# Taps behind splits, gates' sums a projection later, residual sums in tiles of their own, and a last row tile finished on two engines

## The chip, the cores and the metric

The kernel runs on one core of one Trainium2 chip. The metric is the device time of one execution in microseconds (us), as the median of several runs. The core has five engines with a queue each: TensorE (PE, matmuls and transposes), VectorE (DVE), ScalarE (ACT), GpSimd (POOL) and SyncE (SP), which in this kernel issues all DMAs. Each engine takes its instructions strictly in order. They wait for one another through semaphores.

## The reference

One layer of a decoder on 1024 tokens of width 1024, float32: a SwiGLU block, a token mixer, a second SwiGLU block, and a last RMSNorm.

```python
x = x + 0.5 * swiglu(rms_norm(x, ffn1_norm), ffn1_w_gate, ffn1_w_up, ffn1_w_down)
x = x + token_mixer(rms_norm(x, mix_norm), w_in, ...)
x = x + 0.5 * swiglu(rms_norm(x, ffn2_norm), ffn2_w_gate, ffn2_w_up, ffn2_w_down)
return rms_norm(x, final_norm)

def token_mixer(h, ...):
    p = h @ w_in
    ...
    y_a = pool_mixer(u_pool, pool_w, pool_scale)
    y_b = forgetting_attention(q, k, v, z_f, forget_bias)
    y_c = conformer_conv(h_glu, conv_w, conv_b, conv_ln_g, conv_ln_b)
    return concatenate([y_a, y_b, y_c]) @ w_out
```

The pool mixer takes trailing means over 2, 4, 8 and 16 tokens. The attention has 8 heads of 64 and a forget gate per head, whose log sigmoids are summed along the tokens. The convolution is causal and depthwise, 31 taps on 256 channels, on a gated input, with a LayerNorm behind it. The two SwiGLU blocks have 2816 hidden channels.

## The kernel before, in words

Every product is made in three matmuls: each operand is split into a high part (a cast on ACT) and a low part (the rest, a subtraction on DVE), by `split` (L77 to L80) or `split_scaled` (L82 to L85); high by high, high by low and low by high are summed in PSUM. So each operand that PE reads has had one ACT and one DVE instruction. PSUM tiles come from two tags: `bank` (four of 512 columns) and `banks` (two of 1024 columns). SBUF tiles come from four tags, of which `g2` has 11 buffers of 1024 columns; a new tile waits until the last reader of the tile that had its buffer is done, a DMA included.

The order on an engine comes from the order of the code, from a scheduler, and from two helpers: `in_order(start, *engines)` chains all instructions from `start` on in the order in which they are written, and `follow(i, j)` puts one instruction behind another.

The stages are these.

1. The first SwiGLU block (`ffn`, L339 to L562): 77 products of row blocks with pairs of gate and up weights, then 7 groups of down products, whose results are added to the row tiles `xs[0..7]`.
2. The projections of the mixer (from L743 on). `gate(c, h)` makes the gated input of the convolution. `pool_mm` and `pool` make the pooled channels; the latter has some ten DVE instructions, and ends in a split. A loop of 16 value tiles `vp` (256 columns of 8 heads' values, and the gates' logits) follows, then `qk(0)` to `qk(7)`, one per 128 rows of queries or keys, each of 48 matmuls in two halves. `qk` puts the result in a `banks` tile `pp`, and `qk_out` splits it: `qkh` on ACT, `qkl` on DVE. Since there are two such tiles, `qk(i)` can only start when `qkl` of `qk(i-2)` has been read out.
3. The convolution runs beside this on DVE: `conv(n)` issues the next n of 62 taps (31 for each of two channel halves, L719 and L721, tile `ua`). The calls of `conv` stand between the pieces of stage 2. `behind` with `follow` puts the next tap of a half behind the last split of a `pool`.
4. `log_sigmoid` makes the gates' logarithms in place (tile `gates`). `running_sum` turns them (8 transposes into `lp`), sums them on DVE in two scans (tile `fd`), splits the sum (tile `terms`), negates both parts on ACT and stores the rows in DRAM (`augq`, `augk`). It is called in the second half of `qk(2)`, ahead of that projection's `qk_out`. The last taps come in `qk(4)`, the LayerNorm's two means (`channel_mean`) behind `qk(4)` and `qk(5)`.
5. Attention over 64 steps, with output products of finished channels between them.
6. The residual loop (L1176 to L1197): for each of 8 row tiles, 12 matmuls `po`, whose result is added in place to `xs[t]` (L1185 or L1187), a store of `xs[t]` to DRAM (`kept`, L1188), the squares on ACT (`norm2.square`), and one tile later `norm2.scale`, which writes the scaled rows in place into `xs[t]` (L153). The reciprocal root comes from POOL in two small instructions (`inverse`, L147 and L148). From tile 2 on, the scaled rows of the tile two before are transposed (`turn`, tile `tp`, and two splits into `o11` and `o21`).
7. The second SwiGLU block, with weights loaded by `Pair.load` (four loads of two DMAs ahead of stage 6), and `prepare`, which splits them. Both products of `11` come first, then both of `21`. The row tiles are loaded again from `kept`.
8. `finish` (L1218 to L1233) normalises the last row tile in two halves.

In the residual loop before the change, the write of scaled rows has to wait for the store of the same tile:

```python
nc.vector.tensor_tensor(xs[t], o.rearrange("p c x -> p (c x)"), xs[t], op=ALU.add)
nc.sync.dma_start(kept[ts, :], xs[t])
norm2.square(t)
...
norm2.scale(t - 1)
```

## Time and profile before

| what | us |
|---|---|
| median of 3 runs | 1766.65 |
| lowest and highest run | 1762.13, 1768.06 |
| the profiled execution, its own time | 1767.13 |
| its span, first to last instruction | 1765.4 |
| PE busy | 1723.7 (98% of the span) |
| DVE busy | 1216.5 (69%) |
| ACT busy | 690.1 (39%) |
| POOL busy | 164.1 (9%) |
| mean granted clock of PE | 0.991 |

Line numbers, as L153, are those of the kernel before. A row of a timeline gives the start, the duration, engine, line, operation and tiles, and in brackets the idle time of the engine ahead of it with what ended it. Rows that are merged carry a count (x7). Two rows of one engine can overlap by about 0.1 us, so the pitch of equal instructions is a little under the duration of one. PE's rows show 0.39 us for a matmul of 512 columns, while the next begins 0.23 us later. The granted clock is 1.00 at 2.4 GHz and 0.50 at 1.2 GHz.

### The profile page before, as it was taken

Reading aid. Unit: us, or ns where it says so; the run is one execution under the profiler, and the core shown is the slowest. Engines: PE = TensorE matmul, PEld = TensorE weight load, DVE = VectorE, ACT = ScalarE, POOL = GpSimd, SP = SyncE. Lnnn points to the kernel's source line nnn. Section 1 sums busy time; section 2 is a strip of 40 time slices with the busy share of each in tenths; the row PEclk is TensorE's granted clock in tenths of the full one; section 3 lists DMA queues with packets and bytes.
Section 4 is the critical chain, followed back from the end, with each engine's and each line's share of the span. In section 5 each row is a group of like instructions: output and inputs, shape, how many; then the busy total and the mean of one; then the engine's idle time right before and its main releaser. Section 6 shows DMA issues by size and latency. Waiting matters only on the chain.

```text
span 1765.4 us, 21430 instructions
## 1 busy us (share of the span) xinstructions
PE 1723.7 (98%) x8213; PEld 1432.2 (81%) x8214; DVE 1216.5 (69%) x1465; ACT 690.1 (39%) x968; POOL 164.1 (9%) x218
## 2 busy tenths in 40 slices
PE   8999999999999999999899999899999999999998
PEld 6788888888888788898788887788888888888886
DVE  7766666555787674699567786876655566678676
ACT  5433333333334433222545664443333333334343
POOL 3000000000000100221134452100000000000010
PEclk9999999999999999999999999999999999999999
DMA  5333233335723323012563413252333332853342
GB/s 179 109 130 102 89 102 130 99 106 225 282 95 114 102 84 96 1 50 75 170 158 74 121 38 112 68 161 90 104 129 101 102 102 90 334 190 103 106 144 83
DMA packets 173687, 209.69 MB, mean 119 GB/s; under 512 B 9969, under 2 KB 116496, under 8 KB 173584
## 3 DMA queue, kind: packets, MB, share of 16 engines
q1 hardware_dynamic: 173584, 208.31, 36.9%
q8 instruction: 65, 1.06, 0.3%
q14 instruction: 38, 0.31, 0.1%
HBM read 150.87 MB, written 57.41 MB: 118 GB/s over the span
## 4 chain that ended last, share of the span: by engine, by line
PE 48%; DVE 7%; ACT 1%; issue 1%; DMA 1%; POOL 0%; DVEq 0%; POOLq 0%; ACTq 0%
PE pb L354 10%; PE pc L354 6%; PE pa L354 6%; PE po L529 4%; PE po L530 4%; PE po L531 4%; DVE ua L721 4%; PE ysum L1083 2%; PE ptp L1072 2%; PE po L192 1%; PE po L194 1%; PE po L193 1%; PE s L1035 1%; PE s L1036 1%; PE pp L192 1%; PE pp L193 1%
## 5 line engine op out<-in xcount | busy, mean ns | idle before, releaser
L354 PE MATMUL pb<-ot,hi 128*128 128x512 f32 x1056 | 329.9, 393 | 4.4 <-DVE ot L80 4.4
L80 DVE TENSOR_TENSOR lo<-a,hi 128x1024 fp32r<-128x1024 f32 x132 | 161.3, 1223 | 166.8 <-ACT hi L79 166.8
L529 PE MATMUL po<-dh,hh 128*128 128x512 f32 x616 | 240.6, 391 | 1.0 <-DVE x L537 1.0
L530 PE MATMUL po<-dl,hh 128*128 128x512 f32 x616 | 240.1, 390 | 0.0
L531 PE MATMUL po<-dh,hl 128*128 128x512 f32 x616 | 240.0, 390 | 0.0
L354 PEld LDWEIGHTS pb<-ot,hi 128*128 128x128 f32 x1056 | 199.7, 189 | 47.0 <-DVE ot L80 5.8
L79 ACT CAST hi<-a 128x1024 fp32r<-128x1024 f32 x132 | 139.2, 1055 | 250.3 <-PE pa L354 136.7
L354 PE MATMUL pa<-o,hi 128*128 128x512 f32 x704 | 217.7, 390 | 0.0
L354 PE MATMUL pb<-ot,lo 128*128 128x512 f32 x528 | 206.9, 392 | 0.0
L354 PEld LDWEIGHTS pa<-o,hi 128*128 128x128 f32 x704 | 131.6, 188 | 27.1
L147 POOL TENSOR_SCALAR rs<-ss 128x1 f32<-128x1 f32 x32 | 16.9, 529 | 1323.0 <-ACT xn L143 1275.5
L354 PE MATMUL pa<-o,lo 128*128 128x512 f32 x352 | 137.1, 390 | 1.6 <-DVE lo L80 1.6
L529 PEld LDWEIGHTS po<-dh,hh 128*128 128x128 f32 x616 | 116.0, 188 | 25.9 <-DVE x L537 1.8
L531 PEld LDWEIGHTS po<-dh,hl 128*128 128x128 f32 x616 | 115.9, 188 | 24.3
L79 ACT CAST dh<-ds 128x1024 fp32r<-128x1024 f32 (+1 forms) x60 | 58.9, 982 | 195.7 <-DVE ds L395 177.2
L530 PEld LDWEIGHTS po<-dl,hh 128*128 128x128 f32 x616 | 115.9, 188 | 23.8
L354 PEld LDWEIGHTS pb<-ot,lo 128*128 128x128 f32 x528 | 100.0, 189 | 20.8
L354 PE MATMUL pc<-ot,hi 128*128 128x512 f32 x352 | 108.7, 390 | 0.0
L354 PE MATMUL pc<-o,hi 128*128 128x512 f32 x352 | 108.4, 389 | 0.0
L80 DVE TENSOR_TENSOR dl<-ds,dh 128x1024 fp32r<-128x1024 f32 (+1 forms) x60 | 68.1, 1135 | 51.4 <-ACT dh L79 51.3
L80 DVE TENSOR_TENSOR hl<-hr,hh 128x1024 fp32r<-128x1024 f32 x84 | 95.0, 1131 | 2.3 <-PE po L530 0.8
L721 DVE SCALAR_TENSOR_TENSOR ua<-ua,cw 128x1023 f32<-128x1023 f32 (+29 forms) x60 | 88.3, 1491 | 0.6
(243 smaller groups left out, 3173.8 us busy)
## 6 DMA issues: line engine op xcount, KB each, us to landing
hr<-hid SPq DMA_DIRECT2D x70, 512.0 KB
a<-in_ffn_w_gate_dram SPq DMA_DIRECT2D x88, 256.0 KB
a<-in_ffn_w_up_dram SPq DMA_DIRECT2D x88, 256.0 KB
wd<-in_ffn_w_down_dram SPq DMA_DIRECT2D x8, 2048.0 KB
st<-qkd SPq DMA_DIRECT2D x48, 256.0 KB
hid<-ta SPq DMA_DIRECT2D x22, 512.0 KB
hid<-p SPq DMA_DIRECT2D x22, 512.0 KB
x<-in_x_dram SPq DMA_DIRECT2D x16, 512.0 KB
```

Of the source, the lines that this page charges most:

```text
L79: nc.scalar.copy(hi, src)
L80: nc.vector.tensor_tensor(lo, src, f32(hi), op=ALU.subtract)
L192: nc.tensor.matmul(o, wh, mh, start=(i == 0), stop=False)
L193: nc.tensor.matmul(o, wh, ml, start=False, stop=False)
L194: nc.tensor.matmul(o, wl, mh, start=False, stop=(i == n - 1))
L354: nc.tensor.matmul(o, a[:, m, k, :], r[:, b, k, :], start=(start and k == n == 0), stop=(k == 3 and n == 2), skip_group_check=not start,)
L529: nc.tensor.matmul(o[t], hh[:, k, ts], wh[:, k], start=(g == 0 and k == 0), stop=False)
L530: nc.tensor.matmul(o[t], hh[:, k, ts], wl[:, k], start=False, stop=False)
L531: nc.tensor.matmul(o[t], hl[:, k, ts], wh[:, k], start=False, stop=(g == 5 and k == n - 1))
L721: nc.vector.scalar_tensor_tensor(a[:, s:], u[:, :T - s], k, a[:, s:], op0=ALU.mult, op1=ALU.add)
L1072: nc.tensor.transpose(tp[:, k, i, :], items[head * NT + 2 * j + i][0][:, kt * P:(kt + 1) * P], ident)
L1083: nc.tensor.matmul(yp[:, j % 2, :], vs[key_tile(j, u, k)][:, head], pts[:, x % 4, s, k, :], start=(u == 0 and k == 0 and s == 0), stop=(u ...
```

## The change

There are four parts.

Taps. The two `gate` calls of the second channel half ask for 7 taps each instead of 3, and the four places in the pool stage ask for 2 and 1 instead of 4 and 3; `conv(7)` is issued behind `ready(2)`. In the value loop the tap stands behind the split instead of ahead of it.

Gates. `running_sum` keeps the transposes and the scans, and is called after `qk(2)` with its `qk_out`. The split of the sum, the negations and the stores are in `sum_terms`, called in the second half of `qk(3)`. The next tap of each half follows the last scan.

Residual loop. The sum goes to a tile `sums` of its own, out of `g2`. The store reads `sums`, the squares go to the dead `xs[t]` instead of a tile of their own, and `scale` reads `sums` and writes `xs[t]`. Only the first of the two weight halves of each pair is loaded ahead of the loop, the second behind tiles 3 and 5. The weights of both `11` products are prepared in the loop, those of both `21` products behind it. The DVE chain of the loop and of the block's first products is one `in_order` call (`begin` is handed to `ffn`), in both SwiGLU blocks.

Finish. Half 0 is multiplied by the gain on DVE before the root is known, then scaled on ACT and stored from ACT's queue. Half 1 is done on DVE and stored from SP's. The two partial sums of squares are added on POOL in the instruction that adds epsilon, not on DVE.

```diff
         def scale(self, t):
             rs = self.inverse(t)
-            nc.vector.scalar_tensor_tensor(self.xn[t], xs[t], rs, self.gain, op0=ALU.mult, op1=ALU.mult)
+            src = self.src.pop(t, xs[t])
+            nc.vector.scalar_tensor_tensor(self.xn[t], src, rs, self.gain, op0=ALU.mult, op1=ALU.mult)
...
-        def square(self, t):
-            self.xn[t] = xs[t]
+        def square(self, t, src=None):
+            self.xn[t], self.src[t] = xs[t], xs[t] if src is None else src
             self.ss[t] = small.tile([P, 1], F32, name="ss")
-            squares = slot("g2", F32, name="squares")
-            nc.scalar.activation(squares, xs[t], AF.Square, scale=D ** -0.5, accum_out=self.ss[t])
+            squares = slot("g2", F32, name="squares") if src is None else xs[t]
+            nc.scalar.activation(squares, self.src[t], AF.Square, scale=D ** -0.5, accum_out=self.ss[t])
...
-    gate(1, 0, None, lambda: conv(3))
+    gate(1, 0, None, lambda: conv(7))
...
-    gate(1, 1, None, lambda: (conv(3), ready(2)))
+    gate(1, 1, None, lambda: (ready(2), conv(7)))
...
-    pu = pool_mm(0, lambda h: (ready(3), fetch()) if h else conv(4))
+    pu = pool_mm(0, lambda h: (ready(3), fetch()) if h else conv(2))
...
-    pu = pool_mm(1, lambda h: conv(3) if h else ready(4))
+    pu = pool_mm(1, lambda h: conv(1) if h else ready(4))
...
-            conv(1)
             vv = vp[:, :256].rearrange("p (h c) -> p h c", c=HD)
             split(vs[t][:, 4 * j:4 * j + 4, 0, :], vs[t][:, 4 * j:4 * j + 4, 1, :], vv)
+            conv(1)
...
-        terms = slot("g2", F32R, name="terms")
+        behind.update({0: last_instruction(), 1: last_instruction()})
+        sums["fd"] = fd
+
+    def sum_terms():
+        fd, terms = sums["fd"], slot("g2", F32R, name="terms")
         fh, fl, nh, nl = (terms[32 * i:32 * i + HEADS, :] for i in range(4))
         split(fh, fl, fd)
...
-    qk(2, lambda: None, running_sum)
-    qk(3)
+    qk(2)
+    running_sum()
+    qk(3, lambda: None, sum_terms)
...
-    for i in range(4):
-        pairs2[i // 2].load(0, i % 2)
+    for pair in pairs2:
+        pair.load(0, 0)
...
+        sums = slot("g2", F32, name="sums")
...
-                nc.vector.tensor_tensor(xs[t][:, cs], oc, xs[t][:, cs], op=ALU.add)
+                nc.vector.tensor_tensor(sums[:, cs], oc, xs[t][:, cs], op=ALU.add)
         if t % 2 == 0:
-            nc.vector.tensor_tensor(xs[t], o.rearrange("p c x -> p (c x)"), xs[t], op=ALU.add)
-        nc.sync.dma_start(kept[ts, :], xs[t])
-        norm2.square(t)
+            nc.vector.tensor_tensor(sums, o.rearrange("p c x -> p (c x)"), xs[t], op=ALU.add)
+        nc.sync.dma_start(kept[ts, :], sums)
+        norm2.square(t, sums)
...
         if t in (3, 5):
-            pairs2[0].prepare(("11", "21")[t // 2 - 1])
+            pairs2[t // 2 - 1].prepare("11")
+            pairs2[t // 2 - 1].load(0, 1)
...
-    for n in ("11", "21"):
-        pairs2[1].prepare(n)
+    for pair in pairs2:
+        pair.prepare("21")
...
-        xn = slot("g2", F32, name="xn")
+        xn, squares = slot("g2", F32, name="xn"), slot("g2", F32, name="squares")
...
-        r.ss[t] = small.tile([P, 1], F32, name="ss")
-        nc.vector.tensor_tensor(r.ss[t], ss[:, 0:1], ss[:, 1:2], op=ALU.add)
-        rs = r.inverse(t)
-        for c in range(2):
-            nc.vector.scalar_tensor_tensor(xn[:, cs[c]], xs[t][:, cs[c]], rs, r.gain[:, cs[c]], op0=ALU.mult, op1=ALU.mult)
-            nc.sync.dma_start(out[t * P:(t + 1) * P, cs[c]], xn[:, cs[c]])
+        nc.vector.tensor_tensor(xn[:, cs[0]], xs[t][:, cs[0]], r.gain[:, cs[0]], op=ALU.mult)
+        rs = small.tile([P, 1], F32, name="rs")
+        nc.gpsimd.tensor_scalar(rs, ss[:, 0:1], ss[:, 1:2], EPS, op0=ALU.add, op1=ALU.add)
+        nc.gpsimd.tensor_tensor(rs, rs, mhalf, op=ALU.pow)
+        nc.scalar.activation(xn[:, cs[0]], xn[:, cs[0]], AF.Copy, scale=rs)
+        nc.vector.scalar_tensor_tensor(xn[:, cs[1]], xs[t][:, cs[1]], rs, r.gain[:, cs[1]], op0=ALU.mult, op1=ALU.mult)
+        nc.scalar.dma_start(out[t * P:(t + 1) * P, cs[0]], xn[:, cs[0]])
+        nc.sync.dma_start(out[t * P:(t + 1) * P, cs[1]], xn[:, cs[1]])
```

On DVE, from the split of `qk(1)`'s result to that of `qk(2)`'s, before (the last tap ahead of the scans on; `qkl` is a projection's low part, `fd` a scan, `terms` the split of the sum, `ua` a tap):

```order
L721 SCALAR_TENSOR_TENSOR ua<-ua,cw 128x999
L858 SCALAR_TENSOR_TENSOR fd<-one,lp 8x512
L721 SCALAR_TENSOR_TENSOR ua<-ua,cw 128x998
L858 SCALAR_TENSOR_TENSOR fd<-one,fd,lp 8x512
L721 SCALAR_TENSOR_TENSOR ua<-ua,cw 128x997
L80 TENSOR_TENSOR terms<-fd,terms 8x1024
L721 SCALAR_TENSOR_TENSOR ua<-ua,cw 128x996
L85 SCALAR_TENSOR_TENSOR qkl<-pp,qkh 128x1024
```

The same place on DVE now:

```order
L724 SCALAR_TENSOR_TENSOR ua<-ua,cw 128x1005
L85 SCALAR_TENSOR_TENSOR qkl<-pp,qkh 128x1024 x2
L863 SCALAR_TENSOR_TENSOR fd<-one,lp 8x512
L863 SCALAR_TENSOR_TENSOR fd<-one,fd,lp 8x512
L724 SCALAR_TENSOR_TENSOR ua<-ua,cw 128x1004
L724 SCALAR_TENSOR_TENSOR ua<-ua,cw 128x1003
L80 TENSOR_TENSOR terms<-fd,terms 8x1024
L724 SCALAR_TENSOR_TENSOR ua<-ua,cw 128x1002
```

The low parts of `qk(1)` and `qk(2)` now follow each other, with no tap between them and the scans behind them; before, seven taps, both scans, the split of the sum and three more taps stood between the two.

On ACT, at the same place, before (`wh` is a weight's high part, `qkh` a projection's):

```order
L182 CAST wh<-raw 128x1024
L79 CAST terms<-fd 8x1024
L84 ACTIVATE qkh<-pp 128x1024
L864 ACTIVATE terms<-terms 8x1024
L865 ACTIVATE terms<-terms 8x1024
```

And now:

```order
L183 CAST wh<-raw 128x1024
L84 ACTIVATE qkh<-pp 128x1024
L79 CAST terms<-fd 8x1024
L873 ACTIVATE terms<-terms 8x1024
L183 CAST wh<-raw 128x1024
```

The high part of `qk(2)` stood behind the cast that waits for the scans, and now stands ahead of it.

On SP, at the residual loop, before (`a_...` are weight halves, `kept` the stores of the row tiles):

```order
L295 DMA a_8614<-in_ffn_w_up_dram 128x4x128
L295 DMA a_8617<-in_ffn_w_gate_dram 128x4x128
L295 DMA a_8617<-in_ffn_w_up_dram 128x4x128
L295 DMA a_8620<-in_ffn_w_gate_dram 128x4x128
L295 DMA a_8620<-in_ffn_w_up_dram 128x4x128
L1188 DMA kept<-x_3256 128x1024
L1188 DMA kept<-x_3258 128x1024
L1188 DMA kept<-x_3260 128x1024
```

And now:

```order
L297 DMA a_8614<-in_ffn_w_up_dram 128x4x128
L1199 DMA kept<-sums 128x1024 x3
L297 DMA a_8738<-in_ffn_w_gate_dram 128x4x128
L297 DMA a_8738<-in_ffn_w_up_dram 128x4x128
L1199 DMA kept<-sums 128x1024 x2
L297 DMA a_8819<-in_ffn_w_gate_dram 128x4x128
L297 DMA a_8819<-in_ffn_w_up_dram 128x4x128
L1199 DMA kept<-sums 128x1024
```

Two of the four weight halves that stood ahead of the first store now stand behind the third and the fifth.

## Rows read from the trace of the kernel before

**Rows 1.** The page's first part: busy time of each engine, share of the span, instructions.

```profile
PE 1723.7 (98%) x8213; PEld 1432.2 (81%) x8214; DVE 1216.5 (69%) x1465; ACT 690.1 (39%) x968; POOL 164.1 (9%) x218
```

**Rows 2.** Waits of PE: who waited for whom, total us, times, longest.

```profile
PE tp L233 <- DVE x L153: 9.0, 8, 3.3
PE pp L192 <- DVE qkl L85: 6.2, 1, 6.2
```

**Rows 3.** Stretches: length, busy PE, PEld, DVE, ACT, POOL, clock, DMA share, GB/s.

```profile
724.30:735.50 11.20, 11.20 (x51) 9.27 (x50) 0.07 (x2) 2.98 (x4) 5.65 (x3) 1.00 0.00 0
...
844.70:848.70 4.00, 3.96 (x10) 3.16 (x11) 2.31 (x2) 0.74 (x1) 0.00 (x0) 0.51 0.85 266
...
1086.60:1089.90 3.30, 0.04 (x2) 0.02 (x1) 1.36 (x2) 0.00 (x0) 0.18 (x1) 1.00 0.36 148
1089.90:1094.40 4.50, 4.50 (x17) 3.72 (x18) 4.14 (x5) 2.12 (x4) 1.54 (x2) 0.62 0.28 117
...
1138.00:1146.00 8.00, 4.97 (x20) 3.62 (x19) 8.00 (x12) 2.78 (x4) 0.00 (x0) 0.79 0.01 2
```

**Rows 4.** Timeline of PE at the fifth projection, `qk(4)`.

```profile
844.74 0.76 PE L192 MATMUL pp<-xt,wh 128*128 128x512 f32 x1 [6.15 <-DVE qkl L85]
```

**Rows 5.** Timeline of ACT, the same stretch.

```profile
839.86 1.04 ACT L79 CAST terms<-fd 8x1024 fp32r<-8x1024 f32 x1 [17.27 <-DVE fd L858]
840.81 1.01 ACT L84 ACTIVATE qkh<-pp 128x1024 fp32r<-128x1024 f32 x1
```

**Rows 6.** Timeline of DVE, the mixer's projections.

```profile
767.65 3.40 DVE L721 SCALAR_TENSOR_TENSOR ua<-ua,cw 128x1009 f32<-128x1009 f32 x1
...
807.10 2.43 DVE L721 SCALAR_TENSOR_TENSOR ua<-ua,cw 128x1011 f32<-128x1011 f32 x2
...
827.27 9.04 DVE L721 SCALAR_TENSOR_TENSOR ua<-ua,cw 128x1005 f32<-128x1005 f32 x7
...
843.37 1.22 DVE L85 SCALAR_TENSOR_TENSOR qkl<-pp,qkh 128x1024 fp32r<-128x1024 f32 x1
```

**Rows 7.** Chain of work that ended last: start, us, what.

```profile
1082.46 5.94 DMA kept<-x
...
1122.13 0.87 PE tp L233 x8
...
1541.97 5.44 PE pb L354 x24
```

**Rows 8.** Timeline of DVE, the residual loop.

```profile
1088.54 1.28 DVE L153 SCALAR_TENSOR_TENSOR x<-x,rs,gb 128x1024 f32<-128x1024 f32 x1 [3.92 <-DMA kept<-x]
1089.74 1.22 DVE L1187 TENSOR_TENSOR x<-po,x 128x1024 f32<-128x1024 f32 x1
1091.19 1.29 DVE L80 TENSOR_TENSOR o<-tp,o 128x512 fp32r<-128x512 f32 x2 [0.23 <-ACT o L79]
...
1117.09 1.28 DVE L153 SCALAR_TENSOR_TENSOR x<-x,rs,gb 128x1024 f32<-128x1024 f32 x1 [2.38 <-DMA kept<-x]
```

**Rows 9.** Timeline of PE, the residual loop and the block's first products.

```profile
1104.63 1.06 PE L233 MATMUL tp<-ident,x 128*128 128x128 f32 x8 [0.91 <-DVE x L153]
...
1119.56 0.50 PE L354 MATMUL pa<-o,lo 128*128 128x512 f32 x1 [1.61 <-DVE lo L80]
```

**Rows 10.** Timeline of POOL, the residual loop.

```profile
1084.08 0.57 POOL L148 TENSOR_TENSOR rs<-rs,mhalf 128x1 f32<-128x1 f32 x1
...
1103.45 1.12 POOL L147 TENSOR_SCALAR rs<-ss 128x1 f32<-128x1 f32 x1 [5.05 <-ACT squares L228]
```

**Rows 11.** Timeline of the end, DVE, ACT, POOL and SP.

```profile
1758.69 1.28 DVE L153 SCALAR_TENSOR_TENSOR xn<-x,rs,gb 128x1024 f32<-128x1024 f32 x1 [0.21 <-POOL rs L148]
1759.04 0.19 ACT L1225 ACTIVATION_READ_ACCUMULATOR xn<-x 128x1 f32 x1
...
1760.13 0.22 POOL L147 TENSOR_SCALAR rs<-ss 128x1 f32<-128x1 f32 x1 [1.48 <-DVE ss L1229]
...
1761.82 1.00 SPq L1233 DMA_DIRECT2D out_dram<-xn  x2
```

More of the change, by code (lines that the diff above doesn't have):

```diff
@@ L337, in trunk_kernel, with ffn @@
     PLACE = (0, 3, 6, 5, 1, 2, 4)
-    def ffn(ws, xt, pairs, rows, more, late, after, later):
+    def ffn(ws, xt, pairs, rows, more, late, after, later, begin=None):
         hid = dr.tile([7, NQ, P, HALF], F32, name="hid")
@@ L402, in ready @@
             downs[i] = *ops, n
-        begin = len(nc.cur_bb.bb.instructions)
+        first = len(nc.cur_bb.bb.instructions)
         def both(pair, right, o, start):
@@ L497, in ffn @@
             if i == 9:
-                in_order(begin, DVE)
+                in_order(first if begin is None else begin, DVE)
             for q2, n2 in sequence[i:i + (1, 1, 3, 3, 3, 3)[i] if i < 6 else i + 4]:
@@ L561, in ffn @@
                 add(t)
-        in_order(begin, PE)
+        in_order(first, PE)
     ws = ffn1_w_gate[0], ffn1_w_up[0], ffn1_w_down[0]
@@ L615, in trunk_kernel @@
     rows_of(7)
-    in_order(begin, PE, DVE, ACT)
+    in_order(begin, PE, ACT)
+    begin1 = begin
     more1 = norm1.steps()
@@ L844, in log_sigmoid @@
         nc.vector.scalar_tensor_tensor(a, a, 0.0, b, op0=ALU.min, op1=ALU.subtract)
+    sums = {}
     def running_sum():
```

10 lines of the change are left out of this document (5 added, 5 removed).

## The prediction

> **What bounds the kernel now.** I read the busy times first: PE works in 1723.7 of 1765.4 us [rows 1], and no matmul goes away. So only PE's idle time can be won, some 42 us, and the time that PE spends at half clock behind an idle stretch. Next I read who PE waits for [rows 2]. The two largest entries lie where the change is: 9.0 us in eight waits for scaled rows (`tp L233 <- x L153`), the longest, 3.3 us, in the residual loop, and one wait of 6.2 us for a projection's low part (`pp L192 <- qkl L85`). Then I read the stretches [rows 3]: the granted clock is 0.51 just behind the 6.2 us wait and 0.62 behind the 3.3 us wait of the loop, that is, largely 1.2 GHz in place of 2.4. So a long wait costs its length and a slow stretch behind it; shorter ones, of 0.91 and 1.61 us [rows 9], I count at their length alone. Last come the timelines of the two places, which say why DVE was late.
>
> A matmul of 512 columns takes 5.44 / 24 = 0.227 us of PE at full clock, eight transposes 0.87 us [rows 7]. One DVE instruction of 1024 columns, or a pair of 512, takes about 1.2 us from start to start: the rows start at 1088.54 and 1089.74, two taps last 2.43 [rows 6, 8].
>
> **Taps and gates' sums.** Before, PE has done `qk(3)` at about 838.6 and can't start `qk(4)` until 844.74 [rows 4]: it needs the `pp` tile of `qk(2)`, whose low part is read out at 843.37 [rows 6]. `qk(2)` itself was done long before, at 838.6 - 48 x 0.227 - 0.87 = 826.8. Its high part stood on ACT behind the cast of `terms`, which waited 17.27 us for the scans [rows 5], and the scans stood on DVE behind seven taps of 9.04 us [rows 6].
>
> Now `qkh` of `qk(2)` stands ahead of `terms`, and `qkl` ahead of scans and taps. DVE comes there in time: 51 taps precede it where 57 preceded the scans, and six of them go into DVE's idle stretch of 11.20 us from 724.3 on [rows 3]; four more than before are done by the end of the pool stage. Six taps take 7.2 us; beside a cast of POOL one took 3.40 instead of 1.2 [rows 6], and POOL has two casts there, so up to 7.2 + 2 x 2.2 = 11.6 us. That still fits but for 0.4 us. So `qkl` of `qk(2)` comes at 826.8 + 1.0 (ACT) and ends at 829.0, 9.6 us ahead of 838.6. What is late next? Behind it come two scans, two taps, the split of the sum, four taps and `qkl` of `qk(3)`: 10 x 1.2, done at 841.0. PE wants that tile at 838.6 + 10.9 = 849.5. Then a tap, a split, four taps and the last split, at about 850.5 with its cast; the means of the second channel half stand on PE behind four means and 19 matmuls of `qk(5)`, at 849.5 + 5.2 = 854.7. SP now passes the weights of a later projection ahead of the sums' four stores; attention needs the sums' rows only some 40 us later. All of this is off the path by 4 us or more.
>
> So the 6.15 us go, and the slow stretch: 4.0 us at 0.51 cost 4.0 x 0.49 = 2.0. The term is **-8.1**. There is no more to be had here; the other bound is 0, if another wait takes its place.
>
> **Residual loop.** Before, the first scaled rows wait for the store of the same tile, 5.94 us from issue to landing behind four weight pairs [rows 7]; DVE idles 3.92 us [rows 8], and PE idles from 1086.6 to 1089.9 [rows 3]. A second such wait of 2.38 us holds the last tile [rows 8], and through the weights prepared behind it PE waits 1.61 us [rows 9]. Now `scale` reads `sums` as the store does, and waits only for the root, which POOL has ready at 1084.65 [rows 10]. So scaled tile 0 is done by 1086.0, and PE, free at 1086.6, transposes without a wait.
>
> From there DVE is the narrower engine. Between 1086.6 and the transposes of tile 3 it has three sums, three splits of transposes (a pair each), three scalings and one weight: 10 x 1.2 = 12.0, so these transposes start at 1098.6 in place of 1104.63 [rows 9]. PE then has 0.87 + 24 x 0.227 (tiles 6 and 7) + 24 x 0.227 (first product of pair 0) + 0.87 + 12 x 0.227 = 15.3 us to the transposes of `22`, without the 1.61 us wait, because the weights of pair 1 were prepared in the loop. They start at 1113.9 instead of 1122.0. The term is **-8.1**. If DVE were no limit, PE's own work from 1086.6 on is 4 x 0.87 + 60 x 0.227 + 36 x 0.227 + 0.87 = 26.1, which gives 1112.7 and -9.3. The other bound takes back the second wait of 2.38 us three times, for the three sums below: -8.1 + 7.1 = -1.0. I take -8.1, since the DVE rows are those of the same instructions.
>
> The eight stores, the loads and their bytes stay; SP only puts two weight pairs behind the third and fifth store. The second halves are needed with the low parts of `21`, near 1113, and can be issued near 1087 and 1099. The squares in `xs[t]` and the sums in other tiles cost the same instructions. The DVE chain that is now one leaves the order of the first block as it was, on all engines, so that is 0. Behind the transposes of `22` the work is the same on PE, DVE and ACT, and moves as one: the 3.0 us that PE idles there, with a clock of 0.79 [rows 3], stay.
>
> **Finish.** Before: the last sum's squares (to 1759.23), their addition on DVE behind the scaling of tile 6 (1758.69 to 1759.97), POOL at 1760.13, the halves one after the other, the second store leaving at about 1762.4 [rows 11]. Now the multiplication of half 0 stands ahead of the last sum and delays it by 0.6 us, the squares to 1759.85, the scaling of tile 6 to about 1759.1 to 1760.3. POOL's addition then falls beside that scaling; beside such an instruction it took 1.12 us instead of 0.22 [rows 10, 11], as if it had waited for its end. So it ends at 1760.5, the root at 1761.1 (0.57 as in rows 10), both halves side by side at 1761.8: **-0.6**. The Trainium skill (SBUF — State Buffer, SBUF: two separate sides) says that DVE and GpSimd take turns at a shared port pair, each for a whole instruction. By that rule the addition waits as here; without it the term would be -0.9; rows 10 and 11 agree with the rule. The price of a store issued by ACT is in no row. By the nearest, SP's, it is the same; I take from -1.5 (both stores leave at once and land sooner) to +1.0.
>
> **Sum.** -8.1 - 8.1 - 0.6 = -16.8 against the profiled execution's own 1767.13 (span 1765.4 and 1.7 around it), that is 1750.3. The median of the runs is 0.5 below that execution, so I predict 1750.0.
>
> **Rivals.**
>
> *The loop stays half as slow.* Each `sums` tile comes from four free buffers, so the sums of tiles 4, 5 and 6 wait for the stores of tiles 1, 2 and 4. Those stores are issued at about 1085.2 (12 matmuls behind tile 0's at 1082.46), 1087.8 and 1096.2 (one and eight steps of 1.2 from 1086.6), their buffers wanted at 1095.0, 1098.6 and 1103.4 (7, 10 and 14 steps): no wait while landing takes below 9.8, 10.8 and 7.2 us. The 5.94 us [rows 7] speak for a fit with little to spare. If landing takes 11 us, or DVE's twelve and more steps 1.5 us each, about 4 us come back: near 1754.
>
> *The mixer's wait moves on.* The LayerNorm's chain no longer gets the 8 us as slack: its products start about 8 us earlier, the chain itself only some 4, since its sums come in the middle of `qk(6)` now. I count 0.5 to 2 us of slack at the first output products. If the weights of the output come 4 us late, PE waits about 4 us there: also near 1754. Against it: ACT idles for much of that stretch.
>
> *Slower.* Same buffers as in the first rival, but with stores of over 25 us: then the sums of tiles 4 to 6 stand each behind a landing, DVE stands in order, and beyond 7.2 us every microsecond costs one. To lose over 0.3% it must take back 16.8 and 5.3 more, so a landing of 29.3 us; 30 us give 1773. Against it: 5.94 us was with four weight pairs ahead, now there are two.
>
> *It doesn't do what it says.* The scheduler could keep another wait at either place, such as the gain's load for the first scaling. Then one of the two terms goes: 1758; both: no change.
>
> **How the numbers follow.** Forecast 0.73 (1747 to 1753); half a term back, first or second rival, 0.18 (1753 to 1757); a whole term back 0.04 (1758); no change 0.03; slower 0.02. 0.3% is 5.3 us, about what a measurement of this kernel can tell from no change. So faster 0.95, same 0.03, slower 0.02. The range reaches from 8.1 + 9.3 + 1.5 us won, less 3 for the spread of the runs, 1745, to a whole term back, 1758.
>
> **What would show it.** In the profile after: no wait of PE for `qkl`, full clock at `qk(4)`, ACT's cast of `terms` behind `qkh`; in the loop, no wait of a scaling for `kept`, PE's first wait for scaled rows under 0.5 us and that of tile 3 near 1 us, a granted clock of 1.00, and the first transposes of `22` some 8 us earlier against the loop's first sum; the total of PE's waits for `x L153` down by some 3.5 us. It is wrong if DVE shows waits for `kept` at the sums, if PE waits at the first output products of attention, or if the last store leaves over 3 us behind the start of tile 6's scaling.

## The result and the profile after

The changed kernel takes **1748.39 us** (median of four runs, 1747.08 to 1749.43), the kernel before 1767.18 beside it: a ratio of 0.9899, 95% interval 0.9879 to 0.9919. The prediction was 1750.0, range 1745 to 1758, faster. The profiled execution after took 1747.08 us, its span 1745.2; the one before had 1765.4, so there are 20.2 us between the two traces.

PE's busy time fell by 8.1 us with the same matmuls, the first part of the page says, to be held against [rows 1]. Less of it was spent at half clock (a mean granted clock of 0.998, before 0.991):

```profile
PE 1715.6 (98%) x8213; PEld 1425.9 (82%) x8214; DVE 1223.4 (70%) x1464; ACT 690.2 (40%) x969; POOL 170.1 (10%) x218
```

PE's waits after (who waited for whom, total, times, longest). The entry for `qkl` of [rows 2] is gone, and that for scaled rows, now `tp L235 <- x L154`, fell from 9.0 to 3.9 us. Not all of it was in the residual loop, as the prediction reads it: 5.1 us in three waits were, now 1.1 in two, and 3.9 at the start of the first block, now 2.8. What stands first now is in the two blocks themselves:

```profile
PE pb L356 <- DVE ot L80: 4.7, 4, 1.4
PE tp L254 <- DVE ta L364: 4.2, 2, 2.1
PE tp L235 <- DVE x L154: 3.9, 7, 1.0
```

Three stretches after (columns as in [rows 3]). DVE now works in the stretch from 724.3 in which it idled; PE is busy throughout at the place of `qk(4)`, at full clock; the last stretch is the one of [rows 3] at 1138 in its new place:

```profile
724.30:735.50 11.20, 11.20 (x51) 9.27 (x50) 11.06 (x7) 1.77 (x2) 5.55 (x3) 1.00 0.00 0
838.40:844.70 6.30, 6.30 (x29) 5.21 (x29) 6.30 (x5) 1.05 (x1) 2.43 (x1) 1.00 0.52 171
...
1110.00:1125.00 15.00, 11.98 (x64) 9.72 (x63) 12.99 (x17) 7.08 (x10) 0.00 (x0) 1.00 0.00 1
```

The mixer's projections, DVE and then ACT. The low part of `qk(2)` is read out at 824.30 as soon as ACT has its high part, and the scans and the sum's terms follow it; ACT's cast of `terms` stands behind that high part. This answers to [rows 5, 6], where the high part stood behind the cast. The first row is the six taps that fill DVE's idle stretch:

```profile
721.09 13.35 DVE L724 SCALAR_TENSOR_TENSOR ua<-ua,cw 128x1014 f32<-128x1014 f32 x6
...
824.30 1.23 DVE L85 SCALAR_TENSOR_TENSOR qkl<-pp,qkh 128x1024 fp32r<-128x1024 f32 x1 [5.66 <-ACT qkh L84]
825.44 1.20 DVE L863 TENSOR_TENSOR_SCAN fd<-one,lp 8x512 f32<-8x512 f32 x1
...
838.83 1.22 DVE L85 SCALAR_TENSOR_TENSOR qkl<-pp,qkh 128x1024 fp32r<-128x1024 f32 x1
...
823.24 1.02 ACT L84 ACTIVATE qkh<-pp 128x1024 fp32r<-128x1024 f32 x1 [2.45 <-PE pp L195]
828.10 1.05 ACT L79 CAST terms<-fd 8x1024 fp32r<-8x1024 f32 x1 [3.83 <-DVE fd L863]
```

The residual loop, DVE and then PE. The first scaling follows 3.41 us behind the first sum, where it was 7.33 before (1081.21 to 1088.54); no row waits for `kept`, and the transposes of tile 3 have the longest wait that is left, 0.90 us (those of tile 1 have 0.18), and start 17.77 us behind the first sum instead of 23.42. This answers to [rows 8, 9]:

```profile
1069.55 1.23 DVE L1198 TENSOR_TENSOR sums<-po,x 128x1024 f32<-128x1024 f32 x1 [1.27 <-PE po L195]
...
1072.96 1.28 DVE L154 SCALAR_TENSOR_TENSOR x<-sums,rs,gb 128x1024 f32<-128x1024 f32 x1
...
1074.80 1.04 PE L235 MATMUL tp<-ident,x 128*128 128x128 f32 x8
...
1087.32 1.06 PE L235 MATMUL tp<-ident,x 128*128 128x128 f32 x8 [0.90 <-DVE x L154]
...
1102.76 1.03 PE L235 MATMUL tp<-ident,x 128*128 128x128 f32 x8
```

The end, DVE, POOL, ACT's queue and SP's, to be held against [rows 11]. The early multiplication (L1240) stands between PE's last matmul (1736.75) and the last sum; POOL's first instruction for tile 6 (L147), beside that multiplication, takes 0.78 us instead of the 0.22 of [rows 11], and the scaling of tile 6 waits 0.17 us for the root behind it; POOL's addition (L1242) then takes 0.76 us beside that scaling; the halves start together and the stores leave together:

```profile
1737.24 0.69 DVE L1240 TENSOR_TENSOR xn<-x,gb 128x512 f32<-128x512 f32 x1
1737.84 0.68 DVE L539 TENSOR_TENSOR x<-po,x 128x512 f32<-128x512 f32 x1
1738.69 1.29 DVE L154 SCALAR_TENSOR_TENSOR xn<-x,rs,gb 128x1024 f32<-128x1024 f32 x1 [0.17 <-POOL rs L148]
1740.82 0.75 DVE L1245 SCALAR_TENSOR_TENSOR xn<-x,rs,gb 128x512 f32<-128x512 f32 x1 [0.84 <-POOL rs L1243]
...
1737.22 0.78 POOL L147 TENSOR_SCALAR rs<-ss 128x1 f32<-128x1 f32 x1 [1.22 <-ACT xn L143]
...
1739.38 0.76 POOL L1242 TENSOR_SCALAR rs<-ss 128x1 f32<-128x1 f32 x1 [0.72 <-ACT squares L1237]
...
1741.57 0.40 ACTq L1246 DMA_DIRECT2D out_dram<-xn  x1
...
1741.60 0.33 SPq L1247 DMA_DIRECT2D out_dram<-xn  x1
```

**Where the 20.2 us came from.** I cut every trace at four starts: the first matmul of the pool stage (`pu_ps`), the first sum of the residual loop, the last transposes of scaled rows, which are those of `22` (the last of the six groups of the loop, 1102.76 above), and PE's last matmul. The five stretches are in us; the last column is good to 0.05, since the span is given to 0.1:

| kernel | first block | mixer, attention | residual loop | second block | end | median of runs | ratio to before, 95% |
|---|---|---|---|---|---|---|---|
| before | 722.82 | 358.39 | 40.76 | 635.32 | 8.11 | 1767.18 | |
| after | 719.65 | 349.90 | 33.21 | 633.99 | 8.45 | 1748.39 | 0.9899 (0.9879 to 0.9919) |
| mixer's parts alone | 720.38 | 349.86 | 41.62 | 636.74 | 8.00 | 1758.15 | 0.9951 (0.9936 to 0.9966) |
| loop's part alone | 719.56 | 357.78 | 33.22 | 636.75 | 7.99 | 1757.46 | 0.9949 (0.9932 to 0.9965) |
| new end alone | 719.57 | 357.05 | 41.75 | 634.82 | 8.41 | 1766.38 | 1.0003 (0.9994 to 1.0012) |
| after, old end | 719.43 | 349.94 | 33.21 | 633.98 | 8.04 | 1747.27 | 0.9893 (0.9878 to 0.9908) |
| gates' sum alone | 721.36 | 348.44 | 39.39 | 635.67 | 8.04 | 1754.61 | 0.9934 (0.9915 to 0.9953) |
| taps alone | 720.25 | 356.21 | 39.58 | 634.61 | 8.05 | 1763.32 | 0.9981 (0.9969 to 0.9993) |
| sums' tiles alone | 720.16 | 357.83 | 35.34 | 633.96 | 8.01 | 1758.94 | 0.9959 (0.9944 to 0.9974) |
| later loads alone | 721.13 | 358.39 | 33.87 | 635.99 | 8.02 | 1757.83 | 0.9952 (0.9936 to 0.9967) |
| after, multiplication later | 722.86 | 348.33 | 33.20 | 635.63 | 8.18 | 1747.93 | 0.9895 (0.9878 to 0.9911) |
| after, both stores by SP | 721.14 | 349.27 | 33.21 | 636.54 | 8.34 | 1747.49 | 0.9896 (0.9881 to 0.9911) |
| sum, loop, third end | 722.18 | 348.47 | 33.21 | 633.98 | 7.56 | 1747.02 | 0.9893 (0.9878 to 0.9909) |
| after, again | 719.65 | 349.87 | 33.21 | 635.60 | 8.47 | 1747.89 | 0.9895 (0.9880 to 0.9910) |

The mixer gave 8.5 us, the loop 7.55, the end took back 0.35. The other 4.5 are in the two blocks, 3.2 and 1.3, whose instructions the change leaves as they were; the experiments say what they are.

### The profile page after: what moved, and what is told of

Same layout as the page of the kernel before. It is cut to its first block, busy times and chain, and to the rows that moved or that the text cites. A ratio compares the mean times of both kernels' runs of the same rounds, so it can differ in the third digit from the quotient of the medians.

```text
span 1745.2 us, 21440 instructions
## 1 busy us (share of the span) xinstructions
PE 1715.6 (98%) x8213; PEld 1425.9 (82%) x8214; DVE 1223.4 (70%) x1464; ACT 690.2 (40%) x969; POOL 170.1 (10%) x218
## 4 chain that ended last, share of the span: by engine, by line
PE 93%; DVE 3%; ACT 2%; issue 1%; POOL 1%; DMA 0%; SPq 0%; POOLq 0%; ACTq 0%; DVEq 0%
PE pb L356 21%; PE pc L356 13%; PE pa L356 13%; PE po L531 8%; PE po L532 8%; PE po L533 8%; PE ysum L1093 2%; PE ptp L1082 2%; PE pp L195 2%; PE pp L193 2%; PE pp L194 2%; PE po L193 2%; PE po L195 2%; PE po L194 2%; PE s L1045 1%
## 5 line engine op out<-in xcount | busy, mean ns | idle before, releaser
L147 POOL TENSOR_SCALAR rs<-ss 128x1 f32<-128x1 f32 x31 | 18.1, 584 | 1307.8 <-ACT xn L143 1269.0
L724 DVE SCALAR_TENSOR_TENSOR ua<-ua,cw 128x1023 f32<-128x1023 f32 (+29 forms) x60 | 95.2, 1604 | 0.7
```

The source lines that it names most:

```text
L724: nc.vector.scalar_tensor_tensor(a[:, s:], u[:, :T - s], k, a[:, s:], op0=ALU.mult, op1=ALU.add)
```

## Experiments

The kernel before ran beside each group of kernels: medians of 1765.54 (13 runs), 1765.12 (14) and 1765.43 us (7), for the first four, the next four and the last four rows of experiments. The expectations of the first four use slightly other cuts (the loop 1.25 us longer, the end from the last tile's first sum, 1.6 us longer); the differences are the same.

### Do the parts add up?

The first kernel is the one before with the two parts of the mixer:

```
-    gate(1, 0, None, lambda: conv(3))
+    gate(1, 0, None, lambda: conv(7))
...
-    qk(2, lambda: None, running_sum)
-    qk(3)
+    qk(2)
+    running_sum()
+    qk(3, lambda: None, sum_terms)
```

> The kernel before with the taps and the gates' sum moved, nothing else. I read five stretches of every trace: the first block (start to the first matmul of the pool stage's first product), the mixer with attention (to the first residual sum), the residual loop (to the pair of values that the transposes of 22 wait behind), the second block (to the first sum of the last tile), the end. Theory: the parts add up, so this takes 8.1 to 8.5 us out of the mixer's stretch (358.4 before) and nothing out of the loop's (42.0) or the end's (9.7). The first block's 722.8 may come out 3 us shorter, as it did in the change, without any edit there. Rival: the mixer's gain comes only together with the loop's earlier stores and loads, then the mixer's stretch shrinks by less than 7.

Measured: 358.4 became 349.86 in the mixer's stretch, the loop and the end stayed as before, and the first block came out 2.4 us shorter without any edit there. The mixer's gain needs nothing of the loop.

The second has the loop's part alone:

```
-        nc.sync.dma_start(kept[ts, :], xs[t])
-        norm2.square(t)
+        nc.sync.dma_start(kept[ts, :], sums)
+        norm2.square(t, sums)
...
-            pairs2[0].prepare(("11", "21")[t // 2 - 1])
+            pairs2[t // 2 - 1].prepare("11")
+            pairs2[t // 2 - 1].load(0, 1)
```

> The kernel before with the residual loop's part alone (sums in own tiles, squares into the old rows, the second halves loaded and the weights prepared later, one chain of the vector engine). Theory: 7.5 us out of the loop's stretch (42.0 to 34.5), the mixer's stretch stays at 358.4 within 0.5, and the granted clock behind the transposes of 22 is 1.00 or about 0.8, by chance: up to 1.5 us in the second block. Rival: the loop's gain rests on buffers that come free earlier because the mixer is done earlier, then the loop's stretch stays above 38.

Measured: 33.22 in the loop, to a hundredth what the whole change has, with the old mixer ahead of it. Against the old loops (40.76, 41.62 and 41.75, and 39.39 and 39.58 further down) that is 6.2 to 8.5 us.

The third has the new end alone, the fourth the change without it:

```
-        nc.vector.tensor_tensor(r.ss[t], ss[:, 0:1], ss[:, 1:2], op=ALU.add)
-        rs = r.inverse(t)
-        for c in range(2):
-            nc.vector.scalar_tensor_tensor(xn[:, cs[c]], xs[t][:, cs[c]], rs, r.gain[:, cs[c]], op0=ALU.mult, op1=ALU.mult)
-            nc.sync.dma_start(out[t * P:(t + 1) * P, cs[c]], xn[:, cs[c]])
+        nc.vector.tensor_tensor(xn[:, cs[0]], xs[t][:, cs[0]], r.gain[:, cs[0]], op=ALU.mult)
+        nc.gpsimd.tensor_scalar(rs, ss[:, 0:1], ss[:, 1:2], EPS, op0=ALU.add, op1=ALU.add)
...
```

> The kernel before with the new end alone (first half multiplied by the gain early, then scaled by ACT and stored from ACT's queue; the second on the vector engine). Theory: nothing to be measured in the time; the stretch from the last tile's first sum to the end of the span 10.0 us as in the change, where before has 9.7: the early multiplication costs the last sum 0.6 us and the addition on POOL stands beside the scaling of tile 6. Rival (the prediction): it wins 0.6, the stretch is 9.1.

> The changed kernel with the old end. Theory: as fast as the change within 0.3 us by its trace: the end's stretch is 9.7 against 10.0, the mixer's and the loop's stretches as in the change, 349.9 and 34.5. Rival (the prediction): the old end costs 0.6 us, its stretch is 9.7 where the change would have 9.1.

Measured: with the new end the stretch behind the last matmul is 8.41, with the old one 8.04. All eight traces with the old end have 7.99 to 8.11 and the three with the new one 8.41 to 8.47, each within the rounding of the span, so the new end costs 0.4 us. In the median that can't be told: 1.0003 (0.9994 to 1.0012) for the third.

By their medians the mixer alone saves 7.4 us and the loop alone 8.1, together 15.5; the change without the new end saves 18.3. The stretches of the profiled executions, one of each kernel's four, say where 2.8 us more can come from: blocks that nobody edited (719.43 and 633.98 against 720.38 and 636.74, or 719.56 and 636.75). For that see the last experiment.

### Which part of the mixer's change does it?

The gates' sum alone (the second half of the diff above), and the taps alone (its first half, with the later calls of `conv`):

> The kernel before with the gates' sum one step later, the taps where they were. Theory 1 (either part is enough): the projection's low part no longer stands behind scans, so the 6.15 us wait goes, and the stretch of mixer and attention is 350 to 351 where both parts together gave 349.9 and the old order 357 to 358. Four more taps than with both parts are still to be done behind that low part, so the second channel half's split comes some 5 us later, near 856; the LayerNorm's means follow it. Theory 2 (both are needed): those 5 us come out as waits of the tensor engine at the means or at the first output products, and the stretch is 353 or more.

> The kernel before with the taps earlier, the gates' sum where it was. Theory 1 (either part is enough): six taps, 7.2 us, leave the vector engine's queue ahead of the scans, so the scans end near 828 where they ended at 835.5, the high part behind the cast of the sum's terms near 830, its low part near 832, and the tensor engine wants the tile near 835.4 (times on a first block of 719.5): no wait, a stretch of mixer and attention of 350 to 351. Theory 2 (the order on ACT decides, both are needed): the low part still stands behind the sum, a wait of 2 us or more for it stays, and the stretch is 353 or more.

The sum alone gives all of it, 348.44. That is under the 350 to 351 expected, because attention ran at full clock in this trace and not in that of the two parts (349.86); see the last experiment. Its DVE reads the low part of `qk(2)` out when ACT has the high part; the split of the second channel half comes at 857.69, where the mixer's parts together have 851.35, that is 5.4 us later if the difference of the first blocks (721.36 and 720.38) is taken off:

```profile
826.04 1.22 DVE L85 SCALAR_TENSOR_TENSOR qkl<-pp,qkh 128x1024 fp32r<-128x1024 f32 x1 [5.83 <-ACT qkh L84]
...
857.69 1.23 DVE L80 TENSOR_TENSOR al<-ua,ah 128x1024 fp32r<-128x1024 f32 x1 [1.22 <-ACT ah L79]
```

These 5.4 us are nearly covered. PE's waits there have one small entry that the change doesn't show, at the output products:

```profile
PE po L192 <- ACT yt L79: 0.3, 1, 0.3
```

The taps alone give 1 to 2 us (356.21 where the old order has 357.05 to 358.39), and theory 1 fails. PE waits twice for a low part:

```profile
826.97 0.50 PE L192 MATMUL pp<-xt,wh 128*128 128x512 f32 x1 [2.29 <-DVE qkl L85]
...
841.79 0.47 PE L192 MATMUL pp<-xt,wh 128*128 128x512 f32 x1 [2.04 <-DVE qkl L85]
```

DVE, then ACT, say why. The six taps that went into the idle stretch did not leave the queue ahead of the scans: others took their place, since every later call of `conv` takes the next taps of the list. Counted in the traces, 61 taps now stand ahead of the first scan, where 57 did (51 in the change, 47 with the sum alone). The low part of `qk(1)` stands behind six taps of 11.81 us, and the cast of `terms` still waits for the scans and holds back the high part of `qk(2)`:

```profile
813.97 11.81 DVE L721 SCALAR_TENSOR_TENSOR ua<-ua,cw 128x1006 f32<-128x1006 f32 x6
825.70 1.21 DVE L85 SCALAR_TENSOR_TENSOR qkl<-pp,qkh 128x1024 fp32r<-128x1024 f32 x1
...
838.09 1.05 ACT L79 CAST terms<-fd 8x1024 fp32r<-8x1024 f32 x1 [15.82 <-DVE fd L858]
839.05 1.01 ACT L84 ACTIVATE qkh<-pp 128x1024 fp32r<-128x1024 f32 x1
```

So the order of sum and projection is the cause; earlier taps without it only make the queue ahead of the scans longer.

### Which part of the loop's change does it?

The sums' tiles alone, with the four weight pairs loaded ahead of the stores as before; and the later loads and the other order of the prepared weights, with the sums still written into `xs[t]`. The second kernel also has the DVE chain that is one with the block's, which the first doesn't have:

```
+        sums = slot("g2", F32, name="sums")
...
-            nc.vector.tensor_tensor(xs[t], o.rearrange("p c x -> p (c x)"), xs[t], op=ALU.add)
-        nc.sync.dma_start(kept[ts, :], xs[t])
+            nc.vector.tensor_tensor(sums, o.rearrange("p c x -> p (c x)"), xs[t], op=ALU.add)
+        nc.sync.dma_start(kept[ts, :], sums)
```

> The kernel before with the sums in own tiles alone: all four weight pairs still loaded ahead of the stores, the weights prepared in the old order. Theory: the waits of scalings for the store go, 5.9 us of the first and the last tile's, and the wait of 1.6 us for the prepared weights stays: the loop's stretch is 34.5 to 35.5 (33.2 with the whole part, 40.8 to 41.8 before). Rival (buffers): with four pairs of weights held and their transfers ahead of the stores, the sums' tiles wait for landings, the vector engine stands at a sum, and the stretch stays above 37.

```
-    for i in range(4):
-        pairs2[i // 2].load(0, i % 2)
+    for pair in pairs2:
+        pair.load(0, 0)
...
+            pairs2[t // 2 - 1].prepare("11")
+            pairs2[t // 2 - 1].load(0, 1)
```

> The kernel before with the loads and weights of the loop rearranged alone: two pairs ahead of the stores, the others behind, but the sums still written over the old rows, so each scaling waits for its store. Theory: with two pairs fewer ahead of it the first store lands some 2 us earlier, the scaling of tile 0 waits 2 us in place of 3.9, the loop's stretch is 37 to 39.5. Rival: the transfers ahead of the stores are the whole matter, not the shared tile; then it is 34 to 35.

Each alone gives most of it: 35.34 and 33.87, where both together give 33.21 and the old loop 39.4 to 41.8. The first expectation's number (34.5 to 35.5) came true, but not its reason: the wait for the prepared weights, which was to stay at 1.6 us, shrank to 0.20, and a wait for a landing took its place. The second expectation was wrong; its rival (34 to 35) came nearer, but the transfers ahead of the stores aren't "the whole matter", since the sums' tiles alone give most of it too.

With the sums' tiles alone the scalings are free (1081.40, 3.41 us behind the first sum as in the change), but the third sum waits 2.39 us for a store to land, and PE then 1.82 us for the rows of tile 1:

```profile
1085.08 1.22 DVE L1190 TENSOR_TENSOR sums<-po,x 128x1024 f32<-128x1024 f32 x1 [2.39 <-DMA kept<-sums]
...
1088.84 1.06 PE L235 MATMUL tp<-ident,x 128*128 128x128 f32 x8 [1.82 <-DVE x L154]
```

That is the prediction's first rival, and it sets in earlier than the prediction had it: with four weight pairs in place of two in the eleven buffers of the pool `g2`, the sums run out of them at tile 2.

With the later loads alone, each scaling still writes over the tile that its store reads. The first starts 4.59 us behind the first sum (1079.52) instead of 7.33, so PE waits 0.53 us for its rows instead of 3.3, and the granted clock behind that wait is 1.00 where it was 0.62 [rows 3], some 1.7 us more (4.5 x 0.38). The last scaling waits 3.86 us for `kept`, but the first product of pair 0 covers that, with its weights prepared. DVE, then the stretch behind PE's wait:

```profile
1084.11 1.28 DVE L153 SCALAR_TENSOR_TENSOR x<-x,rs,gb 128x1024 f32<-128x1024 f32 x1 [1.17 <-ACT squares L228]
...
1111.92 1.29 DVE L153 SCALAR_TENSOR_TENSOR x<-x,rs,gb 128x1024 f32<-128x1024 f32 x1 [3.86 <-DMA kept<-x]
...
1085.40:1089.90 4.50, 4.36 (x25) 3.55 (x26) 4.27 (x6) 2.12 (x4) 2.12 (x4) 1.00 0.28 117
```

The row puts the wait of 1.17 us down to ACT, but the squares of that tile had ended at 1081.9. The semaphores in the trace settle it: DVE waits there for the store's, whose last signal comes at 1083.90. So the store, issued at 1080.77, landed in 3.1 us, where it took 5.94 behind four pairs [rows 7]. Up to this scaling DVE has the same instructions in the same order as before, so this part of the gain isn't the chain's. Whether the chain has a share in the rest was not run.

### Why the new end doesn't win, and a third end

In the first of these the multiplication stands behind the last sum, in the second both stores are issued by SP:

```
+        last_add = last_vector()
         nc.vector.tensor_tensor(xn[:, cs[0]], xs[t][:, cs[0]], r.gain[:, cs[0]], op=ALU.mult)
+        follow(last_instruction(), last_add)
```

> The changed kernel with the first half's multiplication by the gain put behind the last sum. Read on the stretch from PE's last matmul to the end of the span, 8.4 to 8.5 with the new end, 8.0 to 8.1 with the old. Theory 1 (the early multiplication delays the last sum): the last sum starts 0.5 us behind the last matmul in place of 1.1, the stretch is 7.8 to 7.9. Theory 2 (the two stores that leave together land later than two that leave 0.6 us apart): the last store leaves 0.6 earlier, but the stretch gains less than that, 8.0 to 8.3.

```
-        nc.scalar.dma_start(out[t * P:(t + 1) * P, cs[0]], xn[:, cs[0]])
+        nc.sync.dma_start(out[t * P:(t + 1) * P, cs[0]], xn[:, cs[0]])
```

> The changed kernel with both last stores issued by SP. Theory 1 (early multiplication): the stretch behind the last matmul stays near 8.4 or grows by the 0.4 us that the second issue takes, 8.8. Theory 2 (a store from ACT's queue is slower, or the two together are): it shrinks to 8.0.

The first: the last sum starts at 1740.51, 0.49 us behind the last matmul (1740.02), where the change has 1.09. But only 0.3 us come of it (8.18 instead of 8.45), because POOL's addition, now 0.6 us earlier, meets more of the scaling of tile 6 and takes 1.10 us. DVE, then POOL and SP:

```profile
1740.51 0.68 DVE L539 TENSOR_TENSOR x<-po,x 128x512 f32<-128x512 f32 x1
...
1741.70 1.28 DVE L154 SCALAR_TENSOR_TENSOR xn<-x,rs,gb 128x1024 f32<-128x1024 f32 x1
...
1742.05 1.10 POOL L1247 TENSOR_SCALAR rs<-ss 128x1 f32<-128x1 f32 x1 [0.68 <-ACT squares L1240]
...
1744.61 0.33 SPq L1252 DMA_DIRECT2D out_dram<-xn  x1
```

The addition ends 0.17 us behind the scaling (1743.15 and 1742.98), as in the change it ends 0.16 behind it (1740.14 and 1739.98), whenever it began. By the rule of the Trainium skill (SBUF — State Buffer, SBUF: two separate sides), one of the two engines holds the shared port pair for a whole instruction. These two rows agree.

The second: SP issues the stores at 1744.97 and 1745.40, and the span ends at 1748.5, 3.1 us behind the last issue. In the change both leave at 1741.6 and the span ends 3.6 us later; in the multiplication's kernel likewise (1744.61 and 1748.2). With the old end the second store leaves at 1762.48 and the span ends 2.9 us later. The semaphores in the traces tell the landings: in the change ACT's store lands 2.73 us behind its issue and SP's 2.52, in the old end SP's two 2.07 and 2.03, and here 2.06 and 2.26. So SP's store is late too when both leave at once, and ACT's queue is not the matter, but for 0.2 us at most. The span ends some 0.5 to 0.7 us later behind two halves that leave at the same moment than behind the second of two that leave apart, which is more than the early start had gained:

```profile
1744.97 0.33 SPq L1246 DMA_DIRECT2D out_dram<-xn  x1
1745.40 0.38 SPq L1247 DMA_DIRECT2D out_dram<-xn  x1
```

Theory 2 of the first kernel holds. The second's stretch, 8.34, is near its theory 1 ("stays near 8.4"), but not for that theory's reason: its last store leaves 5.24 us behind the last matmul, 0.4 later than in the change, and lands faster.

The third end keeps the two halves on DVE one after the other, as before, and takes only the addition from DVE, where it stood behind the scaling of tile 6. The rest of this kernel is the gates' sum and the loop's part:

```
-        nc.vector.tensor_tensor(r.ss[t], ss[:, 0:1], ss[:, 1:2], op=ALU.add)
-        rs = r.inverse(t)
+        nc.gpsimd.tensor_scalar(ss[:, 0:1], ss[:, 0:1], EPS, None, op0=ALU.add)
+        rs = small.tile([P, 1], F32, name="rs")
+        nc.scalar.activation(rs, ss[:, 1:2], AF.Identity, bias=ss[:, 0:1])
+        nc.gpsimd.tensor_tensor(rs, rs, mhalf, op=ALU.pow)
```

> The kernel before with the gates' sum moved and the whole loop's part, the taps where they were, and the old end with its addition on ACT in place of the vector engine (the small constant is added to the first half's sum of squares beforehand). Theory: the mixer's stretch 348.4 or 349.9 (with or without a slow stretch in attention), the loop's 33.2, the end's 7.6, since the root no longer stands behind the scaling of tile 6 twice; as fast as the change or up to 1 us faster. Rival: the taps' part is needed once the loop follows directly: then the mixer's stretch is over 351, or the loop's over 34.

The stretches are as expected, 348.47, 33.21 and 7.56 us: the end is 0.9 shorter than the change's. ACT adds at 1739.86, the root follows, and the stores leave apart. One row doesn't show the wait of POOL beside a scaling: the addition of the small constant (L1240), begun 0.05 us behind the scaling of tile 6, takes its 0.22 us, and the scaling 1.31 instead of 1.28. DVE, ACT, POOL and SP:

```profile
1739.22 1.31 DVE L154 SCALAR_TENSOR_TENSOR xn<-x,rs,gb 128x1024 f32<-128x1024 f32 x1 [0.21 <-POOL rs L148]
...
1739.86 0.29 ACT L1242 ACTIVATE rs<-ss 128x1 f32<-128x1 f32 x1
...
1739.27 0.22 POOL L1240 TENSOR_SCALAR ss<-ss 128x1 f32<-128x1 f32 x1
1740.24 0.72 POOL L1243 TENSOR_TENSOR rs<-rs,mhalf 128x1 f32<-128x1 f32 x1 [0.75 <-ACT rs L1242]
...
1741.78 0.99 SPq L1246 DMA_DIRECT2D out_dram<-xn  x2
```

Its median is 1747.02 us, the change's in the same group 1747.89; their ratios to before, 0.9893 (0.9878 to 0.9909) and 0.9895 (0.9880 to 0.9910), can't be told apart. That it is faster rests on the end's stretch alone. It does without the taps' part.

### The change again, and the clock

> The changed kernel once more, on the same chip as the three above. Theory: what it won beyond the sum of its parts was the clock by chance: its stretches are 349.9 or 348.2 (mixer), 33.2 (loop), 8.4 (end); the first block 719.4 or up to 3 us more and the second 634.0 or up to 2.7 more, as slow stretches fall. Rival: the changed order keeps the clock up in the second block, then that is 634.0 again.

The same kernel has 719.65, 349.87, 33.21 and 8.47 us again, each within 0.03, but 635.60 in the second block instead of 633.99. The clock makes that difference. Two stretches each of the change, of the change again and of the third end's kernel (columns as in [rows 3]):

```profile
48.00:60.00 12.00, 9.83 (x55) 8.26 (x56) 10.04 (x14) 3.76 (x4) 0.00 (x0) 1.00 0.03 7
...
1120.00:1132.00 12.00, 9.78 (x54) 8.22 (x55) 10.03 (x14) 3.87 (x4) 0.00 (x0) 1.00 0.03 5
```

```profile
48.00:60.00 12.00, 9.84 (x55) 8.26 (x56) 10.04 (x14) 3.74 (x4) 0.00 (x0) 1.00 0.03 7
...
1120.00:1132.00 12.00, 9.81 (x46) 8.01 (x47) 9.98 (x13) 2.81 (x3) 0.00 (x0) 0.86 0.01 1
```

```profile
48.00:60.00 12.00, 9.96 (x39) 8.06 (x40) 9.86 (x13) 2.63 (x3) 0.00 (x0) 0.72 0.01 2
...
1120.00:1132.00 12.00, 8.97 (x52) 7.31 (x51) 11.02 (x15) 3.75 (x6) 0.00 (x0) 1.00 0.00 1
```

Both stretches hold some 2 to 3 us of idle PE in each of the three; behind it the clock falls in one execution and not in the next. A first block without such a stretch takes 719.4 to 719.7 us (five traces), with it up to 722.9; the second block 633.96 to 633.99 without (four traces), 634.6 to 636.8 with. The mixer has a third place, in attention: 0.79 from 996 to 1004 in the change and in its repetition (349.90 and 349.87), 1.00 in the third end's kernel (348.47). (The 349.27 of the kernel with both stores by SP has a clock of 1.00 there; what its 0.9 us are stays open.) The rival falls: the changed order doesn't keep the clock up in the second block.

So of the 20.2 us between the two profiled executions, 4.5 are such stretches in the trace of before that the trace of after doesn't have, and not the change's. Medians over several runs average them, as far as the runs reach: 1765.43 against 1747.89 in the group that has both kernels, 17.5 us.

## Why the prediction was right, and where it wasn't

**The sum.** -16.8 was predicted; the medians of the last group give -17.5, the first medians -18.8. The forecast case came true, with no new wait. By their stretches in the two profiles the three terms are -8.5, -7.55 and +0.35, together -15.7. What the medians have beyond that is in no term of the sum, and the traces have only the clock in unchanged blocks to put it down to; that the median came as near as 1748.39 to 1750.0 is partly luck. Of the signs that the prediction named, the waits and their order came as said. The last store leaves 2.91 us behind the start of tile 6's scaling (1738.69 to 1741.60), just inside the 3 that would have told against it, and PE's waits for scaled rows fell by 5.1 us, not 3.5.

**Mixer.** Predicted -8.1, measured -8.5 between the two profiles, which both have the slow stretch in attention (a clock of 0.79 from 1008 to 1016 before). The times of the working hold, too: the low part of `qk(2)` was to end at 829.0, and ended at 825.5 in a trace whose first block is 3.2 us shorter. What was not right is the weight of the taps. The prediction lets "six of them go into DVE's idle stretch" as a condition for the low part to come in time; the runs show that without them the stretch is as short (348.44 and 348.47 with clock 1.00 in attention, 348.33 with them). And the second rival's slack was judged too small: "0.5 to 2 us" at the first output products, where a split that comes 5.4 us later costs 0.3. The six taps themselves took 13.35 us, not up to 11.6, and the pooling behind them started 2.1 us later than it would have (734.36, against 735.47 less 3.17 for the first block); no wait of PE came of it.

**Residual loop.** Predicted -8.1, measured -7.55 between the profiles, and -6.2 to -8.5 against the other old loops (39.39 to 41.75). The steps that carry it hold: tile 3's transposes were to start 17.4 us behind the first sum (1098.6 less 1081.21) and start 17.77 behind it, those of `22` 32.7 and 33.21. DVE is the narrower engine there, as said. The step that failed is the cause: "Now `scale` reads `sums` as the store does, and waits only for the root" is true, but would not have been needed. With two fewer weight pairs ahead of the first store and the scaling still bound to it, 2.7 of the 3.9 us went off the first scaling, the clock behind it stayed at 1.00, and the prepared weights covered the wait of the last. The prediction had the later loads only as something that comes in time ("can be issued near 1087 and 1099").

**Finish.** Predicted -0.6, measured +0.35 to +0.4. The mis-sized term is the store: "By the nearest, SP's, it is the same". The last store does leave earlier, 4.85 us behind the last matmul instead of 5.19. But the two then land together and later: the span ends 3.6 us behind the last issue instead of 2.9, which is more than the start had won. The steps up to the halves were near: behind the last matmul the addition was to end at 3.2, the root at 3.8 and the halves at 4.5, and they ended at 3.4, 4.0 and 4.8, so half of the 0.6 was lost on the way. A part of that the prediction didn't have: the early multiplication also stood beside POOL's first instruction for tile 6 (0.78 us instead of 0.22), and the scaling of that tile waited 0.17 us for its root. The bounds, -1.5 to +1.0, held it.

**Behind the loop.** The 3.0 us in which PE idles behind the transposes of `22`, and the clock of 0.79 there, were to "stay". The idle time did (11.98 busy of 15.00), the clock was 1.00 in one trace of the change and 0.86 over 12 us in the other, which costs what 0.79 over 8 us does (12 x 0.14 and 8 x 0.21, both 1.7 us). It is not a property of the kernel that can be carried over from one trace.

**Rivals.** The first (sums that wait for landings) did not occur in the change and did with the loads left early, at 2.39 us. The second (a new wait behind the mixer) shows as 0.3 us without the taps and not at all with them. The slower one and the one without effect did not occur.

## What to carry to other kernels

Look for the cause of a stall where the late instruction stands in its queue, not in the amount of work ahead of it: moving one dependent chain behind a read-out gave all 8 us, moving six taps gave 1 to 2. Where two remedies meet the same wait (a store's shared tile, and the transfers ahead of the store), run each alone before crediting either. And cut two traces at fixed instructions before comparing their ends; more than a fifth of the difference between these two (4.5 of 20.2 us) lay in blocks that were the same.

## What the runs showed that I had not expected

- **The clock behind a short idle stretch is a matter of chance, as far as these traces show.** Behind about 2 us of idle PE, the same instructions ran at a granted clock of 1.00 in one execution and of 0.72 (48 to 60 us) or 0.86 (1120 to 1132 us) over 12 us in another. It costs 0.6 to 3.4 us in a block. The 34 runs of the kernel before reach from 1763.45 to 1769.74 us, and how much of that spread the clock makes is not shown, but two blocks with 0.6 to 3.4 us each could make most of it.
- **Two 256 KB stores that leave at the same moment** end the span 3.6 us later; the second of two that leave 0.4 us apart 3.1, and 0.7 apart 2.9.
- **A one-column root on POOL** (the power, 0.57 us alone) took 0.72 when it began beside a scaling on DVE, and 0.57 beside a sum that reads PSUM (1738.09, in the change). In the kernel before one took 1.40 beside a subtraction on DVE (1108.56). Both slow ones ended 0.43 us behind the DVE instruction. The one-column addition took 0.76 and 1.10 beside the scaling instead of 0.22.
